# Giving out the low parts of the weights one split behind their high parts

## The chip, the core and the metric

The kernel runs on one core of a Trainium2 chip. It is written by hand for the engines TensorE (PE), VectorE (DVE), ScalarE (ACT) and GpSimd (POOL); SyncE (SP) issues most transfers. The metric is device time in microseconds of one execution: 291.53 us as the median of three runs of the kernel before (290.15 to 292.62).

## What is computed

One layer of a decoder trunk for 256 rows of width 1024, in float32. An input projection feeds three mixers: attention over one block of 256 keys (8 heads of 64, with a relative bias), a gated convolution (256 wide) and causal pooling (256 wide). Their outputs pass an output projection, then come a residual, a LayerNorm, a gated MLP of width 2816 with a causal convolution of three taps after the up projection, and a second residual and LayerNorm.

```
h = x @ w_in                                  # q k v | cb cc cx | pin
mix = concat(attention, cb * conv3(cc * cx), pool(pin)) @ w_out
x = layer_norm(ALPHA * x + mix, ln1_g, ln1_b)
up = conv3(x @ w_up) + ffn_conv_b;  u, g = split(up)
out = layer_norm(ALPHA * x + (u * silu(g)) @ w_down, ln2_g, ln2_b)
```

## The kernel before, in words

Large products are taken in the format float32r. To keep float32 accuracy each operand is divided into a high part, its value rounded to float32r, and a low part, the value less the high part. `mm3` (line 150) then issues three matmuls for each product: high by high, high by low, low by high. So each weight is first copied by ACT into `hi` (line 123) and then DVE subtracts `hi` from the raw weight and writes `lo` (line 124). Both lines stand in `split` (line 122), and DVE can start a subtraction only when ACT has finished that copy.

The weights are worked on in **units** of 128 x 1024, listed in `units` (line 75) in the order of their use: `qk` 0 to 7, `v` 0 to 3, `cp` 0 to 7 (the column tiles of the pooling and the convolution), `out` 0 to 7, then for each of the 22 tiles of the MLP `u` j and `g` j (the two halves of the up projection) and, from tile 5 on, a `d` unit of the down projection that belongs to five tiles earlier. I write u1, g1, out7 for ("u", 1), ("g", 1), ("out", 7). u0 and g0 are not divided; they go to PE as they are (`up_first`, line 479).

A raw buffer holds two units (one of the `qk`). There are five (`RB`), filled by SP: `load` (line 96) issues the next transfer when both units of the oldest buffer have been marked by `used` (line 117). `hi` and `lo` have nine buffers each (`WB`).

Nothing is scheduled by the framework: each engine executes its instructions in the order in which the program writes them, and semaphores make it wait for the data. The order comes from the list `blocks` (line 572) and the loop at line 700. For each block the loop writes the block's PE work, then the light work that is due (`late[0]`: evictions, residuals, statistics), then as many splits as `ready` (line 689) allows (`wsplit`, line 130), then `late[1]` (the gate of an MLP tile, the normalising of the softmax). A block may forbid splits (`more=False`); the last block of the output projection and the first two of the three `up_first` blocks do. `ready` looks up to 4 or 7 blocks ahead (`AHEAD`).

The places that the prediction speaks of are these. `w_out_last(0, 0)` runs units out2 to out7 against the columns of `mh` and `ml` (the high and low parts of the mixers' outputs); its last three matmuls need out7 and the second convolution tile, which DVE makes at line 353 (`co`) and `to_mix` divides. After the first LayerNorm, `up_mm(1, 0)` (line 471) uses u1: its third matmul is the first that reads the low part of u1. `ln1_x` (line 463) lets POOL multiply and add the LayerNorm's parameters, four instructions on rows of 1024. `taps` (line 491) does the three taps of an MLP tile, `gate_out` (line 504) multiplies the two halves into `f` and divides it.

Of the kernel before, what the change touches and what calls it, by code (L numbers as in the profile page):

```python
# [10 lines left out]
F32 = mybir.dt.float32  # L11
BF16 = mybir.dt.bfloat16
F32R = mybir.dt.float32r
AF = mybir.ActivationFunctionType
# [3 lines left out]
P = 128  # L18
# [13 lines left out]
H = 1024  # L32
# [25 lines left out]
def trunk(ctx, tc, a_qk, a_v, a_cp, a_out, a_up, a_down, x, par, tab, lnp, out):  # L58
    nc = tc.nc
    cp = ctx.enter_context(tc.tile_pool(name="cp", bufs=1))  # L60
    wp = ctx.enter_context(tc.tile_pool(name="wp", bufs=WB))
# [34 lines left out]
    def load():  # L96

        while len(raws) < len(loads) and (len(raws) < RB or not left[raws[len(raws) - RB]]):
            at, c = loads[len(raws)]
            key = id(at), c  # L100
            n = S + H if at is a_qk else 2 * H
            raw = raw_of[key] = rp.tile([P, n], F32, name="raw")
            if raws:
                nc.sync.dma_start(raw, at[c])
            else:
                nc.sync.dma_start(raw[:, :2 * S], at[c][:, :2 * S])
                nc.sync.dma_start(raw[:, 2 * S:], at[c][:, 2 * S:])
            raws.append(key)
            left[key] = 1 if at is a_qk else 2
# [3 lines left out]
    def part(u):  # L113
        at, c, h = src_of[u]
        return raw_of[id(at), c][:, h * H:(h + 1) * H]

    def used(u):
        at, c, _ = src_of[u]
        left[id(at), c] -= 1
        load()  # L120

    def split(raw, hi, lo):
        nc.scalar.activation(hi, raw, AF.Copy)  # L123
        nc.vector.tensor_sub(lo, raw, hi.bitcast(F32))  # L124

    W = {}
    nsplit = 0
    splits = [u for u in units if u not in (("u", 0), ("g", 0))]

    def wsplit():  # L130
        nonlocal nsplit
        u = splits[nsplit]
        if u[0] == "qk":
            raw = raw_of[id(a_qk), u[1]]
            split(raw[:, :S], xh[:, u[1], :], xl[:, u[1], :])
            w = raw[:, S:]
        else:
            w = part(u)
        hi = wp.tile([P, H], F32R, name="hi")
        lo = wp.tile([P, H], F32R, name="lo")  # L140
        n = (S, H // 2, H)[min(nsplit, 2)]
        for b in range(0 if nsplit else S, H, n):
            cs = slice(b, b + n)
            split(w[:, cs], hi[:, cs], lo[:, cs])
        W[u] = hi, lo
        nsplit += 1
        if u != ("qk", 0):
            used(u)
# [423 lines left out]
    blocks = []  # L572
# [116 lines left out]
    def ready(i):  # L689
        cap = need[min(i + AHEAD[i >= KD + 4 + KD], len(blocks))]  # L690
        if nsplit >= min(len(splits), cap) or nsplit >= WB and free[splits[nsplit - WB]] >= i:
            return False
        at, c, _ = src_of[splits[nsplit]]
        return (id(at), c) in raw_of

    load()
    for _ in range(2):
        wsplit()
    late = [], []
    for i, (pe, _, a, b, now, _, more) in enumerate(blocks):  # L700
        pe()
        if now:
            late = late[0] + a, late[1] + b
            a = b = []
        for f in late[0]:
            f()
        while more and ready(i):
            wsplit()
        for f in late[1]:
            f()  # L710
        late = a, b
# [72 lines left out]
```

## Time and profile before

| | us |
|---|---|
| median of three runs | 291.53 |
| the profiled execution, whole | 291.71 |
| its span, first to last instruction | 289.6 |
| PE busy | 282.8 |
| PE weight loads | 262.8 |
| DVE busy | 220.9 |
| ACT busy | 158.4 |
| POOL busy | 40.6 |

The span is the time from the first to the last instruction in the profiled execution; the 2.1 us between it and 291.71 lie around it. Busy time is the sum over an engine's instructions, and PE's matmuls overlap each other in the pipeline, so the ends of matmuls say less than their starts: a matmul of 256 columns starts 0.117 us after the one ahead of it, though its record lasts 0.28 us, and one of 512 columns 0.228 us after it. Whether PE waits is read from a start that comes later than that.

### The profile page before, as it was taken

The page shows a single profiled execution, that of the slowest core. Times are in us where ns is not written, and L with a number is a line of the kernel's source. Part 1 is how long each engine was busy: PE and PEld are TensorE (multiplying, and loading weights), DVE is VectorE, ACT ScalarE, POOL GpSimd, SP SyncE. Part 2 cuts the span into 40 slices and gives each one's busy share as a digit, 9 for nine tenths or more (in the row PEclk, how much of TensorE's full clock was granted, in tenths as well). Part 3 has the DMA queues.
Part 4 walks back from the last instruction along what each step waited for, and adds up shares of the span by engine and source line. Part 5 has one row for each costly group of instructions (what it writes and reads, how often), then busy time and mean ns, then how long its engine had stood idle before and what let it go on. Part 6 is the DMA issues. An engine that isn't in the chain of part 4 may idle for free.

```text
span 289.6 us, 5052 instructions
## 1 busy us (share of the span) xinstructions
PE 282.8 (98%) x2040; PEld 262.8 (91%) x2040; DVE 220.9 (76%) x384; ACT 158.4 (55%) x263; POOL 40.6 (14%) x42
## 2 busy tenths in 40 slices
PE   8899999999999999999999999999999999999993
PEld 7899779999878999999999999999999999999891
DVE  2774756797958699998988888888667777668584
ACT  3754675828412394366766666666555665655100
POOL 0300004950000289800000000000000000000010
PEclk9999999999999999999999999999999999999998
DMA  6999974143990169284737374848474462200022
GB/s 252 378 354 407 414 272 148 18 145 134 361 359 2 62 231 377 74 285 149 278 147 290 148 285 149 291 148 292 145 290 147 174 224 81 102 2 0 0 76 72
DMA packets 9447, 56.21 MB, mean 194 GB/s; under 512 B 1040, under 2 KB 1552, under 8 KB 3792
## 3 DMA queue, kind: packets, MB, share of 16 engines
q1 hardware_dynamic: 7920, 50.86, 47.1%
q0 software_dynamic: 1072, 4.51, 4.3%
q10 hardware_dynamic: 432, 0.52, 0.5%
q8 instruction: 16, 0.26, 0.4%
q14 instruction: 7, 0.06, 0.1%
HBM read 54.84 MB, written 1.05 MB: 193 GB/s over the span
## 4 chain that ended last, share of the span: by engine, by line
PE 94%; DMA 2%; DVE 1%; ACT 0%; SPq 0%; issue 0%; DVEq 0%
PE bank L152 81%; PE bank L192 7%; PE bank L485 2%; DMA raw<-a_qk 2%; PE bank L267 1%; PE bank L258 1%; PE bank L445 1%; PE bank L227 1%; PE bank L225 0%; DVE xr L565 0%; PE bank L334 0%; DVE xr L560 0%; ACT hi L123 0%; DVE stat L372 0%; DVE xr L385 0%
## 5 line engine op out<-in xcount | busy, mean ns | idle before, releaser
L124 DVE TENSOR_TENSOR lo<-raw,hi 128x1024 fp32r<-128x1024 f32 (+2 forms) x95 | 113.5, 1206 | 24.6 <-ACT hi L123 24.5
L152 PE MATMUL bank<-xh,hi 128*128 128x256 f32 x406 | 114.9, 283 | 0.0
L152 PE MATMUL bank<-xl,hi 128*128 128x256 f32 x406 | 113.6, 280 | 0.0
L152 PE MATMUL bank<-xh,lo 128*128 128x256 f32 x406 | 113.5, 280 | 0.0
L123 ACT ACTIVATE hi<-raw 128x1024 fp32r<-128x1024 f32 (+2 forms) x95 | 95.4, 1019 | 5.2 <-DMA raw<-a_v 4.6
L152 PEld LDWEIGHTS bank<-xh,hi 128*128 128x128 f32 x406 | 76.7, 189 | 1.4 <-issue 0.7
L152 PEld LDWEIGHTS bank<-xl,hi 128*128 128x128 f32 x406 | 76.8, 189 | 0.8
L152 PEld LDWEIGHTS bank<-xh,lo 128*128 128x128 f32 x406 | 76.7, 189 | 0.0
L152 PE MATMUL bank<-hi,mh 128*128 128x512 f32 (+1 forms) x133 | 49.4, 372 | 0.0
L152 PE MATMUL bank<-lo,mh 128*128 128x512 f32 (+1 forms) x133 | 49.2, 370 | 0.0
L152 PE MATMUL bank<-hi,ml 128*128 128x512 f32 (+1 forms) x133 | 49.0, 369 | 0.0
L496 ACT ACTIVATE y<-bank,prm 128x256 f32<-128x256 f32 x44 | 24.6, 560 | 25.8 <-PE bank L152 13.6
L152 PEld LDWEIGHTS bank<-hi,ml 128*128 128x128 f32 x133 | 25.1, 188 | 4.5 <-DVE ml L124 0.2
L410 POOL TENSOR_TENSOR mv<-mv,half 128x1 f32<-128x1 f32 x4 | 2.8, 699 | 186.2 <-DVE mv L409 186.2
L152 PEld LDWEIGHTS bank<-hi,mh 128*128 128x128 f32 x133 | 25.1, 189 | 4.1 <-ACT mh L123 0.4
L152 PEld LDWEIGHTS bank<-lo,mh 128*128 128x128 f32 x133 | 25.1, 188 | 3.5
L497 DVE SCALAR_TENSOR_TENSOR y<-bank,prm,y 128x255 f32<-128x255 f32 x44 | 21.0, 478 | 8.7 <-ACT y L496 8.6
L123 ACT ACTIVATE mh<-f 128x256 fp32r<-128x256 f32 x22 | 9.2, 418 | 24.3 <-DVE f L506 24.3
L498 DVE SCALAR_TENSOR_TENSOR y<-bank,prm,y 128x254 f32<-128x254 f32 x44 | 21.2, 482 | 1.6
L124 DVE TENSOR_TENSOR ml<-f,mh 128x256 fp32r<-128x256 f32 x22 | 11.0, 500 | 10.6 <-ACT mh L123 10.6
L502 ACT ACTIVATE sg<-y 128x256 f32<-128x256 f32 x22 | 9.2, 419 | 13.8 <-DVE y L498 13.8
L192 PE MATMUL bank<-xh,hi 128*128 128x256 f32 x56 | 13.6, 281 | 0.9 <-ACT hi L123 0.9
(105 smaller groups left out, 265.9 us busy)
## 6 DMA issues: line engine op xcount, KB each, us to landing
raw<-a_up SPq DMA_DIRECT2D x22, 1024.0 KB, 4.8
raw<-a_down SPq DMA_DIRECT2D x11, 1024.0 KB, 5.9
raw<-a_qk SPq DMA_DIRECT2D x7, 640.0 KB, 7.8
raw<-a_cp SPq DMA_DIRECT2D x4, 1024.0 KB, 12.7
raw<-a_out SPq DMA_DIRECT2D x4, 1024.0 KB, 4.8
raw<-a_v SPq DMA_DIRECT2D x2, 1024.0 KB, 10.5
lnp<-lnp POOLq DMA_DIRECT2D x4, 512.0 KB, 4.7
bias<-tab POOLq DMA_DIRECT2D x1, 1024.0 KB, 13.3
```

The source lines that it names most:

```text
L123: nc.scalar.activation(hi, raw, AF.Copy)
L124: nc.vector.tensor_sub(lo, raw, hi.bitcast(F32))
L152: nc.tensor.matmul(o, l, r, start=start and i == 0, stop=stop and i == 2, skip_group_check=skip)
L192: nc.tensor.matmul(o, (l if low else h)[:, ws], r[:, k, :], start=False, stop=low and k == KD - 1, skip_group_check=True)
L227: nc.tensor.matmul(s_ps[h][:, P:P + S], qT[r, j, 1], kT[r, j], start=True, stop=True)
L258: nc.tensor.transpose(t_ps[:, i * P:(i + 1) * P], pr[:, i * P:(i + 1) * P], ident)
L267: nc.tensor.matmul(o_ps[s * DH:(s + 1) * DH, t * P:S], v[:, t, h * DH:(h + 1) * DH], pts[h][:, t * S:S + t * P], start=t == 0, stop=t == N ...
L485: nc.tensor.matmul(u_ps[0][:, c:c + P], part(("ug"[s], 0))[:, k * P:(k + 1) * P], xf[:, k, t * P:(t + 1) * P], start=t == 0 and n == 0, st ...
L496: nc.scalar.activation(y, src, AF.Identity, scale=w[2], bias=prm[:, C_FB + c:C_FB + c + 1])
L497: nc.vector.scalar_tensor_tensor(y[:, 1:], src[:, :S - 1], w[1], y[:, 1:], op0=ALU.mult, op1=ALU.add)
L498: nc.vector.scalar_tensor_tensor(y[:, 2:], src[:, :S - 2], w[0], y[:, 2:], op0=ALU.mult, op1=ALU.add)
L502: nc.scalar.activation(ys[j, 2], ys.pop((j, 1)), AF.Silu)
```

## The change

From unit cp4 on (`SKEW`), `wsplit` no longer writes both parts. It first writes the low part that is still owed from the unit ahead, then the high part of its own unit, and notes that unit as owed. `low_part` writes an owed low part and only then calls `used`. The loop calls `low_part` once more behind the splits of a block when that block wrote no split, or when the next block's PE work needs the owed unit. It doesn't do so in blocks with `more=False` that wrote nothing, since the first condition asks for `more`.

```diff
--- before.py
+++ after.py
@@ -127,6 +127,17 @@
     nsplit = 0
     splits = [u for u in units if u not in (("u", 0), ("g", 0))]
 
+    owed = []
+    SKEW = splits.index(("cp", 4))
+
+    def low_part():
+        if owed:
+            u, w, hi = owed.pop()
+            lo = wp.tile([P, H], F32R, name="lo")
+            nc.vector.tensor_sub(lo, w, hi.bitcast(F32))
+            W[u] = hi, lo
+            used(u)
+
     def wsplit():
         nonlocal nsplit
         u = splits[nsplit]
@@ -136,6 +147,14 @@
             w = raw[:, S:]
         else:
             w = part(u)
+        if nsplit >= SKEW:
+
+            low_part()
+            hi = wp.tile([P, H], F32R, name="hi")
+            nc.scalar.activation(hi, w, AF.Copy)
+            owed.append((u, w, hi))
+            nsplit += 1
+            return
         hi = wp.tile([P, H], F32R, name="hi")
         lo = wp.tile([P, H], F32R, name="lo")
         n = (S, H // 2, H)[min(nsplit, 2)]
@@ -704,8 +723,11 @@
             a = b = []
         for f in late[0]:
             f()
+        n = nsplit
         while more and ready(i):
             wsplit()
+        if more and nsplit == n or i + 1 < len(blocks) and any(u == o[0] for u in blocks[i + 1][1] for o in owed):
+            low_part()
         for f in late[1]:
             f()
         late = a, b
```

The order of the instructions on PE, ACT, SP and POOL stays as it was. On DVE the low parts from cp4 on move one place back, each into the place that the next unit's low part had. Three places matter. In the rows, `lo_635<-raw_318,hi_634` reads: a low part, made from a raw buffer and a high part; the number of the high part shows which unit it is.

**DVE, the output projection's units, ahead of the first residual.** Before (out2 to out7 are the six subtractions, out7 is the one with hi_990; the first, with hi_966, is out2):

```order
L348 SCALAR_TENSOR_TENSOR cy_960<-cz_959,prm_104,cy_960 128x254
L124 TENSOR_TENSOR lo_967<-raw_492,hi_966 128x1024
L124 TENSOR_TENSOR lo_971<-raw_492,hi_970 128x1024
L124 TENSOR_TENSOR lo_977<-raw_573,hi_976 128x1024
L124 TENSOR_TENSOR lo_981<-raw_573,hi_980 128x1024
L124 TENSOR_TENSOR lo_987<-raw_699,hi_986 128x1024
L124 TENSOR_TENSOR lo_991<-raw_699,hi_990 128x1024
L353 TENSOR_TENSOR co_1012<-bank_933,cy_960 128x256
L124 TENSOR_TENSOR ml_116<-co_1012,mh_115 128x256
L366 SCALAR_TENSOR_TENSOR xr_1020<-xr_1020,bank_996 128x512
```

After (out1 has hi_913):

```order
L367 SCALAR_TENSOR_TENSOR cy_956<-cz_955,prm_104,cy_956 128x254
L137 TENSOR_TENSOR lo_962<-raw_432,hi_913 128x1024
L137 TENSOR_TENSOR lo_968<-raw_492,hi_966 128x1024
L137 TENSOR_TENSOR lo_972<-raw_492,hi_970 128x1024
L137 TENSOR_TENSOR lo_978<-raw_573,hi_976 128x1024
L137 TENSOR_TENSOR lo_982<-raw_573,hi_980 128x1024
L137 TENSOR_TENSOR lo_988<-raw_742,hi_986 128x1024
L372 TENSOR_TENSOR co_1008<-bank_929,cy_956 128x256
L124 TENSOR_TENSOR ml_116<-co_1008,mh_115 128x256
L137 TENSOR_TENSOR lo_1019<-raw_742,hi_990 128x1024
L385 SCALAR_TENSOR_TENSOR xr_1016<-xr_1016,bank_992 128x512
```

Out1 has come into the row of six, and out7's subtraction stands behind the high and low part of the second convolution tile (`co`, `ml`).

**DVE, unit u1, around the first LayerNorm.** Before, u1's subtraction (hi_1130) stands among the statistics of the second row tile, and behind the four subtractions of the LayerNorm's output (`xl`) come those of g1, u2, g2, u3 and g3:

```order
L366 SCALAR_TENSOR_TENSOR xr_1020<-xr_1020,bank_1004 128x512
L372 BN_STATS stat_119<-xr_1020 128x6 x2
L404 TENSOR_SCALAR stat_119<-stat_119 128x1
L124 TENSOR_TENSOR lo_1131<-raw_917,hi_1130 128x1024
L381 SCALAR_TENSOR_TENSOR xr_1020<-xr_1020,bank_1005 128x512
```

```order
L124 TENSOR_TENSOR xl_75<-xf_1022,xh_74 128x4x128 x4
L124 TENSOR_TENSOR lo_1239<-raw_917,hi_1238 128x1024
L124 TENSOR_TENSOR lo_1245<-raw_974,hi_1244 128x1024
L124 TENSOR_TENSOR lo_1249<-raw_974,hi_1248 128x1024
L124 TENSOR_TENSOR lo_1255<-raw_984,hi_1254 128x1024
L124 TENSOR_TENSOR lo_1259<-raw_984,hi_1258 128x1024
L497 SCALAR_TENSOR_TENSOR y0_1292<-bank_1177,prm_104,y0_1292 128x255
```

After (the five are u1, g1, u2, g2 and u3):

```order
L124 TENSOR_TENSOR xl_75<-xf_1018,xh_74 128x4x128 x4
L137 TENSOR_TENSOR lo_1236<-raw_964,hi_1130 128x1024
L137 TENSOR_TENSOR lo_1240<-raw_964,hi_1238 128x1024
L137 TENSOR_TENSOR lo_1246<-raw_974,hi_1244 128x1024
L137 TENSOR_TENSOR lo_1250<-raw_974,hi_1248 128x1024
L137 TENSOR_TENSOR lo_1256<-raw_984,hi_1254 128x1024
L516 SCALAR_TENSOR_TENSOR y0_1288<-bank_1175,prm_104,y0_1288 128x255
```

The subtraction of u1 has moved behind `xl`, past the second half of the LayerNorm; g3 (hi_1258) has left the row of five.

**DVE, the first MLP tiles.** Before (u4 has hi_1307, g4 hi_1345, u5 hi_1380):

```order
L124 TENSOR_TENSOR lo_1308<-raw_994,hi_1307 128x1024
L506 TENSOR_TENSOR f_1313<-y0_1292,sg_1311 128x256
L124 TENSOR_TENSOR ml_116<-f_1313,mh_115 128x256
L497 SCALAR_TENSOR_TENSOR y0_1341<-bank_1264,prm_104,y0_1341 128x255
L498 SCALAR_TENSOR_TENSOR y0_1341<-bank_1264,prm_104,y0_1341 128x254
L124 TENSOR_TENSOR lo_1346<-raw_994,hi_1345 128x1024
L497 SCALAR_TENSOR_TENSOR y1_1376<-bank_1264,prm_104,y1_1376 128x255
L498 SCALAR_TENSOR_TENSOR y1_1376<-bank_1264,prm_104,y1_1376 128x254
L124 TENSOR_TENSOR lo_1381<-raw_1236,hi_1380 128x1024
```

After:

```order
L137 TENSOR_TENSOR lo_1303<-raw_984,hi_1258 128x1024
L525 TENSOR_TENSOR f_1311<-y0_1288,sg_1309 128x256
L124 TENSOR_TENSOR ml_116<-f_1311,mh_115 128x256
L516 SCALAR_TENSOR_TENSOR y0_1339<-bank_1260,prm_104,y0_1339 128x255
L517 SCALAR_TENSOR_TENSOR y0_1339<-bank_1260,prm_104,y0_1339 128x254
L137 TENSOR_TENSOR lo_1343<-raw_1021,hi_1307 128x1024
L516 SCALAR_TENSOR_TENSOR y1_1372<-bank_1260,prm_104,y1_1372 128x255
L517 SCALAR_TENSOR_TENSOR y1_1372<-bank_1260,prm_104,y1_1372 128x254
L137 TENSOR_TENSOR lo_1376<-raw_1021,hi_1345 128x1024
```

The subtraction of u4 stands behind the gate of tile 0 (`f`, `ml`) and two taps, where g4's stood, and g4's stands where u5's stood.

## Rows read from the trace of the kernel before

**Rows 1.** Chain of waits in order of time: start, length, what.

```profile
104.48 178.21 PE bank L152 x1293
```

**Rows 2.** The page's first part: busy us, share of the span, instructions.

```profile
PE 282.8 (98%) x2040; PEld 262.8 (91%) x2040; DVE 220.9 (76%) x384; ACT 158.4 (55%) x263; POOL 40.6 (14%) x42
```

**Rows 3.** Groups by line: all weights' low parts; busy, mean ns, idle before, releaser.

```profile
L124 DVE TENSOR_TENSOR lo<-raw,hi 128x1024 fp32r<-128x1024 f32 (+2 forms) x95 | 113.5, 1206 | 24.6 <-ACT hi L123 24.5
```

**Rows 4.** Timeline of DVE, 50 to 83: start, length, line, operation, [idle before, releaser].

```profile
50.30 1.22 DVE L124 TENSOR_TENSOR lo<-raw,hi 128x1024 fp32r<-128x1024 f32 x1 [2.05 <-ACT hi L123]
...
71.78 0.41 DVE L271 CAST mh<-bank 128x256 fp32r<-128x256 f32 x1
...
72.57 0.41 DVE L344 TENSOR_TENSOR cz<-bank,cx 128x256 f32<-128x256 f32 x1
...
74.39 6.89 DVE L124 TENSOR_TENSOR lo<-raw,hi 128x1024 fp32r<-128x1024 f32 x6
81.21 0.42 DVE L353 TENSOR_TENSOR co<-bank,cy 128x256 f32<-128x256 f32 x1
82.11 0.43 DVE L124 TENSOR_TENSOR ml<-co,mh 128x256 fp32r<-128x256 f32 x1 [0.48 <-ACT mh L123]
```

**Rows 5.** Timeline of PE, 68 to 83: attention's last product; into out7.

```profile
68.73 1.52 PE L267 MATMUL bank<-pt,v 128*64 128x256 f32 x16
...
81.72 0.39 PE L152 MATMUL bank<-hi,ml 128*128 128x512 f32 x1
82.13 0.50 PE L152 MATMUL bank<-hi,mh 128*128 128x512 f32 x1
82.47 0.40 PE L152 MATMUL bank<-lo,mh 128*128 128x512 f32 x1
```

**Rows 6.** Timeline of DVE, 92 to 129.

```profile
92.77 1.22 DVE L124 TENSOR_TENSOR lo<-raw,hi 128x1024 fp32r<-128x1024 f32 x1
...
102.24 2.48 DVE L124 TENSOR_TENSOR xl<-xf,xh 128x512 fp32r<-128x512 f32 x4
104.64 5.75 DVE L124 TENSOR_TENSOR lo<-raw,hi 128x1024 fp32r<-128x1024 f32 x5
...
112.89 3.33 DVE L124 TENSOR_TENSOR lo<-raw,hi 128x1024 fp32r<-128x1024 f32 x1
116.14 2.62 DVE L506 TENSOR_TENSOR f<-y,sg 128x256 f32<-128x256 f32 x1
119.24 2.06 DVE L124 TENSOR_TENSOR ml<-f,mh 128x256 fp32r<-128x256 f32 x1 [0.49 <-ACT mh L123]
...
122.13 1.22 DVE L124 TENSOR_TENSOR lo<-raw,hi 128x1024 fp32r<-128x1024 f32 x1
...
127.61 1.23 DVE L124 TENSOR_TENSOR lo<-raw,hi 128x1024 fp32r<-128x1024 f32 x1
```

**Rows 7.** Timeline of PE: the first matmul that reads u1's, u4's, u5's low part.

```profile
104.56 0.28 PE L152 MATMUL bank<-xh,lo 128*128 128x256 f32 x1
...
121.36 0.28 PE L152 MATMUL bank<-xh,lo 128*128 128x256 f32 x1
...
126.96 0.28 PE L152 MATMUL bank<-xh,lo 128*128 128x256 f32 x1
```

**Rows 8.** Timeline of POOL: the first of the four instructions of `ln1_x`.

```profile
102.71 9.95 POOL L464 TENSOR_TENSOR xr<-xr,lnp 128x1024 f32<-128x1024 f32 x1 [3.19 <-DMA lnp<-lnp]
```

**Rows 9.** Timeline of SP: the issue behind g4's low part.

```profile
123.37 0.33 SPq L104 DMA_DIRECT2D raw<-a_down  x1
```

**Rows 10.** The page's DMA issues, the down projection's loads: KB each, us to landing.

```profile
raw<-a_down SPq DMA_DIRECT2D x11, 1024.0 KB, 5.9
```

**Rows 11.** Timeline of ACT: the high part of d2, first reader of that load.

```profile
144.64 1.05 ACT L123 ACTIVATE hi<-raw 128x1024 fp32r<-128x1024 f32 x1
```

**Rows 12.** Timeline of DVE: the low part of the last gate, tile 21.

```profile
269.97 0.43 DVE L124 TENSOR_TENSOR ml<-f,mh 128x256 fp32r<-128x256 f32 x1 [0.48 <-ACT mh L123]
```

**Rows 13.** Timeline of PE: the first matmul that reads that gate.

```profile
271.36 0.39 PE L152 MATMUL bank<-hi,mh 128*128 128x512 f32 x1
```

## The prediction

> **What bounds the kernel now.** I read the chain of waits first. From 104.48 us to 282.69 us it is one piece, 1293 matmuls of line 152 [rows 1]: PE follows itself and waits for nobody, so in the MLP the time is PE's own. The page's busy times say the same from outside, PE 98% of the span against 76% for DVE [rows 2]. Next come the groups by line. The subtraction that makes a low part has 95 instances, 1206 ns each, and 24.5 us of idle time ahead of them that ACT's copies end [rows 3]. This is the wait that the change can take away. It lies on DVE, which isn't the bound, so its 24.5 us are not a gain as they stand. What can move the time is only this: whether a low part reaches PE before PE asks for it. So I read last the timelines of DVE and PE at the places where the order changes.
>
> One rule speaks against reading PE as full. The Trainium skill, "Perfetto Trace Analysis", section "Identifying the Most-Contended Engine", says that matmul busy time is a bad measure and that the busy share of the weight loads is a good one. By it PE would stand at 91% [rows 2], with 9% of 289.6 us, 26 us, to be had, and up to the whole 24.5 us could come back. The chain has no link in the MLP that isn't PE, so I go by the chain.
>
> **The change, part by part.** It adds and removes no instruction. Each low part from cp4 on moves into the place on DVE that the next unit's had. Nearly everywhere a low part is ready many microseconds early, and a place later costs nothing. Three places are tight.
>
> *Out7, at 82 us.* The low part goes behind `ml` of the second convolution tile. `ml` ran from 82.11 to 82.54 [rows 4]; a subtraction of 1.22 us that overlaps its end by 0.08 ends at 83.68. PE read out7's low part at 82.47 [rows 5]. If DVE kept its times, PE would stand 83.68 - 82.47 = 1.2 us longer: the upper bound. But DVE comes here earlier. The subtraction at 50.30 had waited 2.05 us for ACT [rows 4], and the ones behind it waited too; their places now hold units whose copies are done. How much of that arrives at 82 us is limited by attention's last product on PE, which starts at 68.73 and lasts 1.52 us, to 70.25 [rows 5]. The second CAST reads it and ran at 71.78 [rows 4], so DVE gains 1.5 us at most from there on. From that CAST through `cz` (72.57), the six subtractions (74.39, 6.89 us long) and `co` (81.21) it is one run without idle time [rows 4], so the gain arrives whole. Then out7's low part ends at 82.2. `mh` of that tile comes 1.5 us earlier as well, and PE's own wait for it falls away: the step from 81.72 to 82.13 was 0.41 us and the next 0.34 us [rows 5], against 0.228 us for a matmul of 512 columns, together 0.3 us lost. PE would then read the low part at 82.2 instead of 82.47. I take -0.25 us, nearer the end that has all of the 1.5 us, because every operation in between is DVE's own; the bounds are -0.3 and +1.2.
>
> *U1, at 104.5 us.* Its low part was made at 92.77 [rows 6], 12 us before PE's first reading of it at 104.56 [rows 7]. No splits are written around the LayerNorm, so the owed part is given out only behind `xl`: at 104.64, as the first of the five that run there [rows 6]. With 1.22 us it ends at 105.86, and PE, at its third matmul of the tile, waits 105.86 - 104.56 = 1.3 us. What is queued behind it on PE is the whole MLP. On DVE nothing waits longer, since the five subtractions take the same 5.75 us. The taken-out subtraction at 92.77 frees 1.2 us of DVE there, but the residual behind it waits for PE's next product anyway; I cost it at nothing. Nothing else can hide the 1.3 us; above it lies only the lock told of below, under it nothing down to 1.2 us.
>
> *U4, at 121 us.* DVE is late here: the subtraction at 112.89 took 3.33 us instead of 1.22, `f` 2.62 us and `ml` 2.06 us [rows 6], while POOL ran `ln1_x`, whose first instruction alone took 9.95 us [rows 8]. U4's low part was made at 112.89, ending 116.22; now it takes g4's place, 122.13 to 123.35 [rows 6]. PE asked for it at 121.36 [rows 7], so against DVE's clock PE is now 2.0 us late, of which 1.3 us have been lost at u1 already: another 0.7 us. The units behind ask for less: u5's low part falls into the place at 127.61, ends at 128.84 [rows 6], and PE asked at 126.96 [rows 7], 1.9 us. So 2.0 us is the largest delay, and the later ones are covered by it. DVE's idle waits for ACT further on vanish, but PE has nothing to gain there.
>
> *Transfers.* `used` comes a place later, so SP's queue issues later; each issue stands behind DVE's subtraction. The load behind g4's low part went out at 123.37 [rows 9], takes 5.9 us [rows 10], and ACT first reads it at 144.64 [rows 11]: 15 us of cover against a delay of about 2 us. I cost it at nothing; without that cover ACT's copies, then PE, would be 2 us later per load.
>
> *The tail.* The last low part now stands ahead of tile 21's gate, so its `ml`, which ended at 270.40 [rows 12], ends up to 1.2 us later, at 271.6, plus PE's own delay of 1.75 us where DVE follows PE. PE first reads that gate at 271.36 plus the same 1.75 us and its low half two matmuls, 0.46 us, later [rows 13]. With the 1.2 us whole it would cost 0.2 us at the low half; part of it falls into DVE's idle time ahead of `f`, so I cost it at nothing.
>
> **The sum.** -0.25 + 1.3 + 0.7 = +1.75 us on the profiled execution's 291.71 us: 293.5 us. That execution lies 0.2 us above the median of the three runs, so in terms of the median I predict **293.3 us**.
>
> **The rivals** (times against the median, 291.53).
>
> *DVE doesn't arrive early at out7.* If a POOL operation or an eviction on ACT sets DVE's pace between 50 and 72 us, out7 costs up to +1.2 and the sum is 1.2 + 2.0 = +3.2, 294.7 us. For it: ACT and DVE answer each other there. Against it: the run without idle time behind the CAST. 15%.
>
> *POOL takes its turn ahead of u1.* POOL's first instruction stands waiting from 102.71 [rows 8] and seems to be let in only when DVE's subtractions end. If it gets in between `xl` and u1's low part, that part takes 3.33 us as at 112.89, 2.1 us more, and PE waits 3.4 us at 104.56. The turn is then spent (POOL has four), so u4 is no later than before. Sum -0.25 + 3.4, about +3.2 us: 294.7 us. It decides if DVE pauses at all behind `xl`; in the trace it doesn't. 7%. The Trainium skill, "SBUF — State Buffer", section "Who interferes with whom", calls the port pair that DVE and GpSimd share an exclusive lock, held for a whole instruction, and says that the order of issue decides who blocks. By that rule the price is such a turn, and the trace agrees: 9.95 us of POOL beside DVE's subtractions, then 3.33 us for one of DVE's.
>
> *U1 costs its 1.3 us, u4 nothing.* If DVE is 0.7 us quicker between 104 and 122 us (a turn of POOL that falls elsewhere), the sum is about +1.05: 292.6 us. 13%.
>
> *Nothing is lost, or a little gained.* Only out7's 0.3 us come back, 291.2 us. It needs PE to have slack that its starts hide; the chain shows none. 4%. By the rule on weight loads, told above, there is such slack; were all of the 24.5 us [rows 3] on the path, the time would be 267 us. 1%.
>
> The forecast has the remaining 60%, with a range of its own of 292.8 to 293.9 us.
>
> **The range.** 291.8 to 295.0 us: it takes in the first three rivals with some scatter, since the three runs lie 2.5 us apart, and leaves out the last and the far ends. A measurement of this kernel can tell about 1% from no change, 2.9 us, so slower by over 1% begins at 294.4 us: the first two rivals, 22%, and a tail of the forecast, together 25%. Faster by over 1% needs 288.6 us, 2%. Within 1%: 73%.
>
> **What the changed profile would show.** PE: a step of about 1.4 us instead of 0.117 ahead of u1's first low-part matmul, released by line 137 on DVE, and one of 0.8 us at u4's; no longer a step of 0.41 ahead of out7. DVE: the idle time ahead of the low parts by ACT's copies nearly gone after 50 us, which would be no gain. The chain would show DVE pieces at about 105 and 123 us. I would be wrong if PE waits at units beyond u5, if a load comes late, or if the matmuls themselves run at another pace.

## The result, and the profile after

The change takes 293.61 us (292.13 to 293.95) against 291.53 us (290.15 to 292.62): a ratio of 1.0058, 95% interval 1.0037 to 1.0078, or 1.1 to 2.3 us slower. The prediction was 293.3 us, in a range of 291.8 to 295.0. The profiled execution took 293.83 us, with a span of 291.8 us against 289.6.

The first part of the program, up to the scores of the attention, ends earlier or later from execution to execution: the first matmul of cp0 starts between 41.73 and 45.44 us in those shown here, though the change begins four units behind it. To compare single executions I use **the stretch**: from that matmul to the last matmul of line 171 (line 152 before). Before it runs from 43.74 to 282.39 us, 238.65 us; after from 43.63 to 284.57, 240.94 us: 2.29 us more.

The page of the change, its busy line and three of its groups (busy us, mean ns, idle time before them and its releaser):

```profile
PE 282.4 (97%) x2040; PEld 261.9 (90%) x2040; DVE 221.1 (76%) x384; ACT 158.8 (54%) x263; POOL 39.3 (13%) x42
...
L171 PE MATMUL bank<-xh,lo 128*128 128x256 f32 x406 | 113.6, 280 | 1.5 <-DVE lo L137 1.5
...
L137 DVE TENSOR_TENSOR lo<-raw,hi 128x1024 fp32r<-128x1024 f32 x76 | 94.8, 1258 | 0.3 <-ACT hi L154 0.3
...
L516 DVE SCALAR_TENSOR_TENSOR y<-bank,prm,y 128x255 f32<-128x255 f32 x44 | 21.1, 479 | 20.7 <-ACT y L515 20.6
```

Each engine executes as many instructions as in [rows 2]. The 76 owed low parts wait 0.3 us for ACT, and the 19 others, made as before, 10.5 us; before, all 95 waited 24.5 us [rows 3]. So 13.7 us of waits are gone. The taps of line 516, however, wait 20.6 us for ACT now. The view of waits of the kernel before has for the same taps (us in total, times, longest):

```profile
DVE y L497 <- ACT y L496: 8.6, 8, 1.1
```

So 12 us of DVE's idle time have moved from the subtractions to the taps, since DVE still follows PE's pace; and PE has a wait for a low part that it did not have.

The chain of waits of the change, in order of time (start, length, what):

```profile
81.02 1.23 DVE lo L137
82.29 8.91 PE bank L171 x38
...
104.64 1.17 DVE lo L137 x2
...
122.16 1.15 DVE lo L137
123.35 161.51 PE bank L171 x1147
```

Where [rows 1] had one piece of PE from 104.48, the chain now goes through the low parts of out7 (81.02), u1 (104.64, the first of two) and u4 (122.16). Between u1 and u4 it has no matmul: it stays with DVE's own row, but for two short pieces of ACT, and only from 123.35 on is it PE alone. The timeline of PE at these places (start, length, line, operation, idle before):

```profile
81.62 0.39 PE L171 MATMUL bank<-hi,ml 128*128 128x512 f32 x1
81.84 0.39 PE L171 MATMUL bank<-hi,mh 128*128 128x512 f32 x1
82.29 0.50 PE L171 MATMUL bank<-lo,mh 128*128 128x512 f32 x1
82.63 0.40 PE L171 MATMUL bank<-hi,ml 128*128 128x512 f32 x1
...
104.36 0.28 PE L171 MATMUL bank<-xl,hi 128*128 128x256 f32 x1
105.83 0.39 PE L171 MATMUL bank<-xh,lo 128*128 128x256 f32 x1 [1.19 <-DVE lo L137]
106.05 0.28 PE L171 MATMUL bank<-xh,hi 128*128 128x256 f32 x1
...
111.35 0.28 PE L171 MATMUL bank<-xh,hi 128*128 128x256 f32 x1
...
119.83 0.28 PE L171 MATMUL bank<-xh,hi 128*128 128x256 f32 x1
...
122.78 0.28 PE L171 MATMUL bank<-xl,hi 128*128 128x256 f32 x1
123.35 0.39 PE L171 MATMUL bank<-xh,lo 128*128 128x256 f32 x1 [0.30 <-DVE lo L137]
123.58 0.28 PE L171 MATMUL bank<-xh,hi 128*128 128x256 f32 x1
```

Read it by the distances of the starts, nominally 0.117 us at 256 columns and 0.228 at 512. At u1 a step of 1.47 and then one of 0.22 us: 1.35 + 0.10 = 1.45 us lost. At u4 0.57 and 0.23: 0.45 + 0.11 = 0.56 lost. At out7 0.45 and 0.34: 0.22 + 0.11 = 0.33 lost, where before 0.41 and 0.34 had lost 0.29 [rows 5]; so 0.04 more, not 0.25 less. Together +2.05 us. The remaining 0.24 us of the 2.29 lie in the pace: from 111.35 to 119.83 three halves of MLP tiles (24 matmuls each) took 8.48 us, 2.827 each, and from about 106 to 134 us ten of them ran so, against 2.80 us each before (104.56 to 121.36 [rows 7] are six). The view by windows of that stretch (length, busy us and instructions of PE, weight loads, DVE, ACT and POOL, granted clock, share of DMA, GB/s) has the clock at its full level:

```profile
108.00:130.00 22.00, 21.70 (x184) 21.50 (x184) 20.16 (x24) 10.65 (x17) 13.92 (x6) 1.00 0.68 250
```

The timeline of DVE of the change, which answers to [rows 4, 6, 12]:

```profile
69.54 0.42 DVE L290 CAST mh<-bank 128x256 fp32r<-128x256 f32 x1 [1.00 <-PE bank L286]
...
72.96 6.90 DVE L137 TENSOR_TENSOR lo<-raw,hi 128x1024 fp32r<-128x1024 f32 x6
...
80.68 0.42 DVE L124 TENSOR_TENSOR ml<-co,mh 128x256 fp32r<-128x256 f32 x1 [0.48 <-ACT mh L123]
81.02 1.22 DVE L137 TENSOR_TENSOR lo<-raw,hi 128x1024 fp32r<-128x1024 f32 x1
...
104.56 5.76 DVE L137 TENSOR_TENSOR lo<-raw,hi 128x1024 fp32r<-128x1024 f32 x5
...
112.78 3.38 DVE L137 TENSOR_TENSOR lo<-raw,hi 128x1024 fp32r<-128x1024 f32 x1
...
122.08 1.22 DVE L137 TENSOR_TENSOR lo<-raw,hi 128x1024 fp32r<-128x1024 f32 x1
...
272.50 0.43 DVE L124 TENSOR_TENSOR ml<-f,mh 128x256 fp32r<-128x256 f32 x1 [0.48 <-ACT mh L123]
```

From the six subtractions to `ml` DVE is 1.43 us earlier than in [rows 4]. U1's low part is the first of the five at 104.56, and u4's is the one at 122.08; the long one at 112.78 is the one beside POOL, as in [rows 6].

The issue that stood behind g4's low part, on SP, answers to [rows 9], and the high part of d2 on ACT to [rows 11]:

```profile
125.41 0.33 SPq L104 DMA_DIRECT2D raw<-a_down  x1
```

```profile
144.48 1.05 ACT L154 ACTIVATE hi<-raw 128x1024 fp32r<-128x1024 f32 x1
```

The issue is 2.0 us later than in [rows 9], and its reader not later at all.

### The profile page after: what moved, and what is told of

Its sections match the earlier page's. It is cut to its first block, busy times and chain, and to the rows that moved or that the text cites. A ratio compares the mean times of both kernels' runs of the same rounds, so it can differ in the third digit from the quotient of the medians.

```text
span 291.8 us, 5017 instructions
## 1 busy us (share of the span) xinstructions
PE 282.4 (97%) x2040; PEld 261.9 (90%) x2040; DVE 221.1 (76%) x384; ACT 158.8 (54%) x263; POOL 39.3 (13%) x42
## 4 chain that ended last, share of the span: by engine, by line
PE 81%; DVE 12%; DMA 2%; ACT 2%; issue 1%; SPq 0%; POOL 0%; DVEq 0%; ACTq 0%
PE bank L171 71%; PE bank L211 7%; DVE lo L137 6%; DMA raw<-a_qk 2%; PE bank L277 1%; DVE xf L476 1%; DVE f L525 1%; DVE xl L124 1%; DVE ml L124 1%; ACT hi L154 1%; PE bank L246 1%; DVE y L517 0%; PE bank L286 0%; DVE xr L455 0%; DVE y L516 0%
## 5 line engine op out<-in xcount | busy, mean ns | idle before, releaser
L171 PE MATMUL bank<-xh,hi 128*128 128x256 f32 x406 | 114.1, 281 | 0.0
L137 DVE TENSOR_TENSOR lo<-raw,hi 128x1024 fp32r<-128x1024 f32 x76 | 94.8, 1258 | 0.3 <-ACT hi L154 0.3
L154 ACT ACTIVATE hi<-raw 128x1024 fp32r<-128x1024 f32 x76 | 78.7, 1047 | 0.0
L516 DVE SCALAR_TENSOR_TENSOR y<-bank,prm,y 128x255 f32<-128x255 f32 x44 | 21.1, 479 | 20.7 <-ACT y L515 20.6
L124 DVE TENSOR_TENSOR lo<-raw,hi 128x1024 fp32r<-128x1024 f32 (+2 forms) x19 | 19.3, 1040 | 10.6 <-ACT hi L123 10.5
L123 ACT ACTIVATE mh<-f 128x256 fp32r<-128x256 f32 x22 | 9.2, 418 | 24.5 <-DVE f L525 24.5
L123 ACT ACTIVATE hi<-raw 128x1024 fp32r<-128x1024 f32 (+2 forms) x19 | 16.6, 901 | 4.7 <-DMA raw<-a_v 4.2
```

The lines of the kernel that those rows point to most:

```text
L137: nc.vector.tensor_sub(lo, w, hi.bitcast(F32))
L154: nc.scalar.activation(hi, w, AF.Copy)
L171: nc.tensor.matmul(o, l, r, start=start and i == 0, stop=stop and i == 2, skip_group_check=skip)
L516: nc.vector.scalar_tensor_tensor(y[:, 1:], src[:, :S - 1], w[1], y[:, 1:], op0=ALU.mult, op1=ALU.add)
```

## The experiments

My theory: a low part costs what it is late at PE, and the change makes three of them late; nothing else in it costs or gives anything. Rivals: a part of the cost is spread over all units, or VectorE's freedom from ScalarE's copies is worth something once nothing is late. All ratios are against the kernel before. A stretch is that of the one profiled execution, and 0.1 us of it is scatter: the kernel before, u1 alone and from u8 have the same order around out7, and PE's steps lost 0.29, 0.22 and 0.17 us there.

| | ratio, 95% | stretch, us | against before, us |
|---|---|---|---|
| the change | 1.0058, 1.0037 to 1.0078 | 240.94 | +2.29 |
| u1 alone | 1.0065, 1.0037 to 1.0093 | 240.08 | +1.43 |
| u1 early | 1.0012, 0.9983 to 1.0041 | 239.75 | +1.10 |
| POOL written late | 1.0058, 1.0029 to 1.0087 | 240.80 | +2.15 |
| up to out7 | 0.9991, 0.9966 to 1.0017 | 238.70 | +0.05 |
| POOL held back | 1.0038, 1.0013 to 1.0062 | 240.11 | +1.46 |
| from u8 | 0.9998, 0.9971 to 1.0024 | 238.55 | -0.10 |
| out7 in time | 0.9990, 0.9963 to 1.0017 | 238.48 | -0.17 |
| all three mended | 0.9967, 0.9944 to 0.9990 | 238.47 | -0.18 |

**U1 alone.** Only u1's low part is given out one split behind; every other unit as before.

```diff
-        if nsplit >= SKEW:
+        if u == ("u", 1):
             low_part()
...
             return
+        low_part()
         hi = wp.tile([P, H], F32R, name="hi")
```

> Every unit is divided as in the kernel before, but u1's low part alone is given out one split late, behind the LayerNorm's last subtractions. Theory (the lateness against DVE's clock counts, and u1's is 1.35 us with 0.1 us for PE's restart): the step into u1's first low-part matmul is about 1.4 us instead of 0.117 us, u4 and the units behind it cause no wait, since their low parts keep their places on DVE (DVE runs one subtraction, 1.15 us, late and PE 1.45 us late). Span 1.45 us longer than before, 291.1 us. If the slightly slower pace of the matmuls behind u1 in the changed kernel (a tile half in 2.825 us instead of 2.80 us) comes from PE's having stopped, it is here too and adds up to 0.2 us. Rival (the whole loss comes from skewing the MLP's units): under 0.7 us.

Timeline of PE:

```profile
103.41 0.28 PE L172 MATMUL bank<-xl,hi 128*128 128x256 f32 x1
104.87 0.39 PE L172 MATMUL bank<-xh,lo 128*128 128x256 f32 x1 [1.19 <-DVE lo L137]
105.10 0.28 PE L172 MATMUL bank<-xh,hi 128*128 128x256 f32 x1
...
110.35 0.28 PE L172 MATMUL bank<-xh,hi 128*128 128x256 f32 x1
...
118.75 0.28 PE L172 MATMUL bank<-xh,hi 128*128 128x256 f32 x1
```

One unit of 76 gives the whole step of 1.46 us and the 0.23 behind it, 1.45 us lost, and the stretch is longer by just that, 1.43 us. U4 does not wait. Three halves from 110.35 to 118.75 take 8.40 us, 2.80 each, in spite of the wait ahead of them.

**U1 early.** The change, but u1's low part is given out as soon as its block's splits are written.

```diff
-        if more and nsplit == n or i + 1 < len(blocks) and ...
+        if owed and owed[0][0] == ("u", 1) or more and nsplit == n or i + 1 < len(blocks) and ...
             low_part()
```

> The changed kernel, but u1's owed low part is given out at the end of its own block, where the kernel before had it, ahead of the LayerNorm. Theory (the largest lateness against DVE's clock counts): u1's wait is gone, and with four instead of five subtractions behind the LayerNorm DVE is 1.15 us earlier, so u4's low part ends at about 122.2 us against PE's 121.36 us: the step at u4 grows from 0.57 us to about 0.95 us, and the span is 0.9 us to 1.0 us longer than before, 1.2 us shorter than the changed kernel's. Rival (waits add up one by one): u4 keeps its 0.45 us and the span is 0.6 us longer than before.

Timelines of PE and of DVE:

```profile
119.30 0.28 PE L171 MATMUL bank<-xl,hi 128*128 128x256 f32 x1
120.33 0.39 PE L171 MATMUL bank<-xh,lo 128*128 128x256 f32 x1 [0.74 <-DVE lo L137]
120.55 0.28 PE L171 MATMUL bank<-xh,hi 128*128 128x256 f32 x1
```

```profile
102.70 4.62 DVE L137 TENSOR_TENSOR lo<-raw,hi 128x1024 fp32r<-128x1024 f32 x4
...
109.78 3.36 DVE L137 TENSOR_TENSOR lo<-raw,hi 128x1024 fp32r<-128x1024 f32 x1
...
119.05 1.22 DVE L137 TENSOR_TENSOR lo<-raw,hi 128x1024 fp32r<-128x1024 f32 x1
```

U1's wait is gone, and the step into u4 grows from 0.57 to 1.03 us: 0.91 + 0.10 = 1.0 us lost, a little over the 0.95 us that I expected of the step. Were waits added up one by one, the step would have stayed at 0.57. So the largest lateness counts once, and what u1 had not taken u4 takes. It is not the whole 2.0 us, since DVE has one subtraction fewer behind `xl` (four, 4.62 us, instead of five, 5.76) and arrives at u4's low part that much earlier. The ratio alone would not settle this; its interval holds no change too.

**POOL written late.** `ln1_x` and the loads that stand behind it on POOL are written at tile 14 instead of tile 0, to take POOL's turns away from DVE.

```diff
-            block(seq(), (), [L(ln_rows, 0), L(taps, 0, 0), L(taps, 0, 1), L(ln1_x, 0), L(ln1_x, 1),
-                              L(ln_rows, 1)], gate)
+            block(seq(), (), [L(ln_rows, 0), L(taps, 0, 0), L(taps, 0, 1)], gate)
...
-            block(L(up_mm, j, 0), [("u", j)], [L(taps, j, 0)])
+            block(L(up_mm, j, 0), [("u", j)],
+                  [L(taps, j, 0)] + [L(ln1_x, 0), L(ln1_x, 1), L(ln_rows, 1)] * (j == 14))
```

> The changed kernel, but POOL's four instructions that multiply and add the first LayerNorm's parameters, and the loads behind them, stand at MLP tile 14 instead of tile 0. Theory (u4 is late because DVE lost 6 us to POOL's turns): the subtraction, f and ml at 113 to 121 us take 1.2, 0.4 and 0.4 us, u4 causes no wait, u1 keeps its step of 1.47 us; span 1.45 us to 1.6 us longer than before, 0.6 us shorter than the changed kernel's. At tile 14 POOL's turns slow DVE by the same 6 us, and the low parts are far enough ahead there. Rival (u4's place alone makes it late): u4's step stays at 0.57 us and the span is 2.2 us longer than before.

Timeline of POOL:

```profile
104.48 9.90 POOL L483 TENSOR_TENSOR xr<-xr,lnp 128x1024 f32<-128x1024 f32 x1 [3.23 <-DMA lnp<-lnp]
```

The edit missed its aim. POOL has nothing else in its queue, so the instruction starts when its data is there, as in [rows 8], wherever the program writes it: 59.04 us behind the first matmul of cp0 here, 58.97 us before. The run is a second look at the change: steps of 1.46 us at u1 and 0.69 at u4, and the halves at 2.80 us.

**POOL held back.** The same, with a tiny copy on POOL ahead of it that reads tile 14's `y`.

```diff
+    def pool_gate():
+        nc.gpsimd.tensor_copy(tmp("pg")[:, :1], ys[14, 0][:, :1])
...
-                  [L(taps, j, 0)] + [L(ln1_x, 0), L(ln1_x, 1), L(ln_rows, 1)] * (j == 14))
+                  [L(taps, j, 0)] + [pool_gate, L(ln1_x, 0), L(ln1_x, 1), L(ln_rows, 1)] * (j == 14))
```

> The changed kernel, but POOL's four instructions on the first LayerNorm's rows, and the loads behind them, are held back by a one-column copy on POOL that reads the taps of MLP tile 14, so that POOL works beside DVE at about 200 us and not at 113 to 121 us. Measured from cp0's first matmul to the last matmul, which is 238.65 us before and 240.94 us in the changed kernel (the start ahead of it differs by up to 2 us between executions). Theory (u4 is late because DVE lost 6 us to POOL's turns): the subtraction, f and ml behind the taps of tile 0 take 1.2, 0.4 and 0.4 us, the step of 0.57 us to 0.69 us into u4's first low-part matmul falls to 0.117 us, u1's step of 1.46 us stays, and the stretch is 240.1 us. Rival (u4's place on DVE alone makes it late): the step stays and the stretch is 240.8 us.

Timelines of POOL and of DVE:

```profile
209.23 0.19 POOL L483 COPY pg<-y 128x1 f32<-128x1 f32 x1 [110.20 <-ACT y L518]
209.37 2.40 POOL L486 TENSOR_TENSOR xr<-xr,lnp 128x1024 f32<-128x1024 f32 x1
```

```profile
112.36 1.22 DVE L137 TENSOR_TENSOR lo<-raw,hi 128x1024 fp32r<-128x1024 f32 x1
114.27 0.42 DVE L528 TENSOR_TENSOR f<-y,sg 128x256 f32<-128x256 f32 x1 [0.69 <-ACT sg L524]
115.18 0.43 DVE L124 TENSOR_TENSOR ml<-f,mh 128x256 fp32r<-128x256 f32 x1 [0.48 <-ACT mh L123]
```

With POOL away DVE's three instructions take 1.22, 0.42 and 0.43 us instead of 3.38, 2.62 and 2.07, and POOL's multiplication 2.40 us instead of 9.99. U4 waits no more, u1's step of 1.46 us remains, and the stretch is at +1.46. So DVE and POOL held each other up between 103 and 121 us, and that is what makes u4 late. At tile 14 POOL's turns lengthen DVE's instructions likewise (two subtractions of 2.74 and 2.52 us, `f` 2.62 and `ml` 2.08 us between 210 and 221 us), and no step of PE is longer there: the low parts are early enough. The Trainium skill, "SBUF — State Buffer", section "Who interferes with whom", has for this that a DVE instruction with two inputs in SBUF and a GpSimd instruction that reads SBUF exclude each other for the length of an instruction. The trace agrees: each of the three is longer by 1.6 to 2.2 us, less than one turn of POOL's 2.40.

**Up to out7, and out7 in time.** The first has the skew from cp4 up to the last unit ahead of u1, and the old order from u1 on. The second adds that out7's low part is written ahead of the convolution's late work.

```diff
-        if nsplit >= SKEW:
+        if SKEW <= nsplit < splits.index(("u", 1)):
...
             return
+        low_part()
         hi = wp.tile([P, H], F32R, name="hi")
...
+        if owed and owed[0][0] == ("out", 7):
+            low_part()
         for f in late[0]:
```

> Low parts a split late from cp4 to out7 only; from u1 on as in the kernel before. Theory: DVE comes 1.4 us earlier to the second convolution tile, PE waits 0.33 us for out7's low part where it had waited 0.3 us for that tile's high part, and nothing else moves: the same span as before, 289.6 us, within 0.2 us. Rival 1 (the changed kernel's DVE time is worth something to PE): 0.3 us shorter. Rival 2 (part of the 2.2 us is lost ahead of the LayerNorm): 0.3 us or more longer.

> Low parts a split late from cp4 to out6 only, and out7's given out ahead of the second convolution tile, as in the kernel before; from u1 on as before. Theory: DVE comes there 1.4 us earlier, out7's low part is ready at 80.9 us and the convolution tile's high part at 81.8 us, just when PE asks for it at 81.84 us, so that the 0.3 us that PE loses there before go away: from cp0's first matmul to the last 238.35 us. Rival (the waits at out7 aren't DVE's): 238.65 us. As a time of the whole execution 0.1% would not be told from no change.

The first gives +0.05 us: PE's steps are 0.44 and 0.34 us there, as in the change. Of the second, PE, DVE and PE's weight loads (PEld):

```profile
81.33 0.49 PE L172 MATMUL bank<-hi,mh 128*128 128x512 f32 x1
81.65 0.40 PE L172 MATMUL bank<-lo,mh 128*128 128x512 f32 x1
```

```profile
72.45 8.03 DVE L137 TENSOR_TENSOR lo<-raw,hi 128x1024 fp32r<-128x1024 f32 x7
```

```profile
81.31 0.19 PEld L172 LDWEIGHTS bank<-hi,mh 128*128 128x128 f32 x1 [0.25 <-ACT mh L123]
```

Out7's low part is the seventh of the row now and long done at 81.65; the step of 0.32 us loses 0.09 where before 0.29 were lost, and 0.22 and 0.17 in the two other executions with the old order there. So the early arrival of DVE, as such, is worth 0.1 to 0.2 us; the expectation had 0.3, but the weight load of `mh` still waits for ACT. The change spends the gain again by putting out7's low part last.

**From u8.** The skew only from u8 on, behind all three places, where low parts are made long before PE reads them.

```diff
-    SKEW = splits.index(("cp", 4))
+    SKEW = splits.index(("u", 8))
```

> The change from unit u8 on instead of from cp4 on. DVE's waits for ACT's copies there, 16 of 0.5 us, go away. Theory (a low part that comes early enough costs and gains nothing): from cp0's first matmul to the last matmul 238.65 us within 0.1 us, the same time as before; DVE's idle time moves to the taps. Rival (the change slows or quickens PE also where low parts are early): more than 0.3 us either way.

The view of DVE's waits (us in total, times, longest):

```profile
DVE y L516 <- ACT y L515: 19.4, 13, 1.8
DVE lo L124 <- ACT hi L123: 16.5, 12, 3.9
```

Sixteen of the 28 waits for ACT's copies are gone, 8.0 of 24.5 us, the taps' waits grew by 10.8 us instead, and the time did not move: the -0.10 us are about what PE's steps at out7, ahead of the skew, differ by. In the MLP of the kernel before, from 104.50 to 271.00 us, weight loads are busy for 157.72 of the 166.50 us. By the rule on weight loads that the prediction told of ("Perfetto Trace Analysis", section "Identifying the Most-Contended Engine", of the Trainium skill) the 8.8 us that are left would be room to take some of it; the trace disagrees.

**All three mended.** The change with u1 early, POOL held back and out7 in time: the three edits above together, so no new lines.

> The whole skew from the fifth conv tile on, with its three late places mended at once: out7's low part is written ahead of the late ops of its block, u1's low part is given out as early as its high part allows, and POOL's first row of the layer norm is held back to tile 14. Theory (all that the change costs is the lateness of out7's, u1's and u4's low parts, and it has nothing to give beyond out7's 0.2 us, since TensorE waits for no other low part before): the stretch from the first conv matmul to the last matmul 238.4 to 238.5 us against 238.65 of the kernel before and 240.94 of the change; the ratio to the kernel before 0.998 to 1.000; no step of TensorE over 0.4 us ends on a low part. Rival (VectorE's freedom from ScalarE's copies is worth something of its own once nothing is late): 237.5 us or less, ratio under 0.996. Rival (the skew has a cost of its own, such as a slower pace or a later load): 239.5 us or more, ratio over 1.003.

Chain of waits, its piece of the MLP:

```profile
103.07 178.21 PE bank L171 x1293
```

The MLP is one piece of PE again, of 1293 matmuls and of the very 178.21 us of [rows 1], although the owed low parts wait 0.3 us for ACT here too. No step over 0.33 us ends on a low part, and the stretch is 238.47 us, where the theory had 238.4 to 238.5. The ratio of 0.9967 lies a little below what I expected of it, and its interval reaches to 0.9990; the stretch accounts for 0.18 us of the 1 us, and out of the rest, which lies outside the stretch or in the scatter of the starts, I make nothing. Its ratio is the lowest of the versions; that it beats the kernel before by more than 0.1% is not shown.

## Why the prediction was right, and where a term was off

- **What bounds the kernel**: right. PE's own row of matmuls sets the time, and in the MLP idle time of DVE is worth nothing: shown by the skew from u8, and by the mended version.
- **U1, +1.3 us**: the place, the releaser and the size are right. It is 1.45 us, by 1.35 of waiting and 0.10 for the slower step behind it, which I had not counted. U1 alone shows that it is this one unit.
- **U4, +0.7 us**: 0.56 us in the change, 0.57 + 0.11 = 0.68 in the run with POOL written late. In the first PE ran at 2.827 us per half, so it asked for u4 0.15 us later and waited 0.12 us less. That the largest lateness counts once, and that POOL causes this one, is shown by u1 early and by POOL held back. The rival in which u4 costs nothing is out.
- **Out7, -0.25 us**: the term that was mis-sized; +0.04 came. PE's wait for `mh` did go. The step that failed is "PE would then read the low part at 82.2 instead of 82.47", for two reasons. DVE gained less against PE than the 1.5 us: it came 1.43 us earlier, but PE too was 0.11 us earlier in this execution (43.63 against 43.74 us at cp0), so the gain is 1.32 us. I had counted from the second CAST and the end of attention's last product; but the first CAST already waits, for the first half of that product (69.54 above), where before it did not:

```profile
70.99 0.42 DVE L271 CAST mh<-bank 128x256 fp32r<-128x256 f32 x1
```

And I had the end of the low part as the moment from which nothing is lost. PE could have read it at 81.84 + 0.228 = 82.07; the low part ended at 82.24, PE read it at 82.29, and the matmul behind it came 0.34 us later instead of 0.228. The rival in which DVE does not arrive early (+1.2) is out.

- **POOL's turn ahead of u1**, a rival: it did not come; DVE made no pause behind `xl`, and u1's low part took its 1.22 us.
- **Transfers and tail at nothing**: right. The issue at 125.41 had cover enough, and the last gate's `ml` ends at 272.93, when PE is still at work on earlier products: before, PE read that gate at 271.36 [rows 13], and all of PE is 2.2 us later here.
- **Not in the sum**: the slower pace of ten halves in the profiled execution of the change, 0.24 us. The prediction had named another pace as a sign that it would be wrong. It did not come again in the run with POOL written late, which has the same waits, nor with u1 alone, u1 early or POOL held back. With the granted clock at 1.00, what it was stays open.

The sum came out at 1.75 us against 2.05 us by PE's steps, 2.29 us by the stretch and 2.1 us by the medians. That is less than the scatter of single runs. In part it is luck: u1 cost 0.15 us more and u4 0.14 us less than predicted, and the two cancel. What is left between 1.75 and 2.29 us is out7 (0.29) and the pace (0.24). The measurement also tells more than the 1% that the prediction allowed it: its interval is 0.2% to either side, and shows the change to be slower.

## What to carry to other kernels

Before you move work off an engine's wait, see whether that wait is on the path: the 13.7 us of waits that DVE lost here were worth 0.2 us at most, since PE had hardly ever stood for them. Then look for the few consumers that have no slack, above all where a stretch forbids the step that would hand the work out: one unit out of 76 cost two thirds of the loss. Several late arrivals for one engine don't add up; the largest lateness counts, and mending the first only uncovers the next.

## What the hardware showed besides

- After a wait PE loses another 0.1 us: the matmul behind the one that waited starts 0.22 us later instead of 0.117 at 256 columns, and 0.34 instead of 0.228 at 512. The weight loads of the change at u1 show where it goes:

```profile
105.83 0.19 PEld L171 LDWEIGHTS bank<-xh,lo 128*128 128x128 f32 x1 [1.39 <-DVE lo L137]
105.94 0.19 PEld L171 LDWEIGHTS bank<-xh,hi 128*128 128x128 f32 x1
```

In the running row each weight load starts with the matmul ahead of its own, 0.12 us before it. The load that waited starts only with its own matmul, at 105.83, whose record lasts 0.39 us instead of 0.28, and the next load starts 0.11 us behind it, for the matmul at 106.05. By these rows the 0.1 us is a load that could not be made ahead. With out7 in time the same longer step stands behind a matmul that was not late itself (81.33): its weight load had waited, to 81.31, where one made ahead would have started at 81.10.

- Where DVE subtracts without a pause, POOL does not get in: its multiplication, 2.40 us long at 209.37 in the run with POOL held back, lasted 9.99 us beside five subtractions, which took their usual time (5.76 us), and only the single instructions of DVE behind them paid.
- An instruction of POOL that is written later in the program runs no later if nothing stands ahead of it in POOL's queue; it takes a dependence to move it (104.48 us when written late, 209.23 us with the copy that reads late data).
